# A chunked linear-attention layer in which every second 128-token tile lies backwards and two tiles share one score product per level

## The chip, the cores and the metric

The kernel runs on one core of one Trainium2 chip. The metric is the device time of one execution in microseconds. Engines are named as the profile names them: PE (TensorE matmul), PEld (TensorE weight load), DVE (VectorE), ACT (ScalarE), POOL (GpSimd), SP (SyncE, here the queue that issues most DMAs).

## The reference: what is computed

One layer of a hybrid decoder, for a prompt of 1024 tokens and for 8 sample sequences of 4 tokens, model width 1024, all in float32. After a norm, one wide projection feeds two branches: a gated linear recurrence (RG-LRU, 10 blocks of 128 channels, with a causal convolution of width 4), and gated linear attention (GLA, 4 heads, keys of 128, values of 256). Gates merge the branches; a SwiGLU feed-forward net follows. The attention is what the change touches; cut to the core it is

```python
bc = jnp.cumsum(gc, axis=2)
decay = jnp.exp(jnp.where(mask, bc[:, :, :, None, :] - bc[:, :, None, :, :], -jnp.inf))
att = jnp.einsum('bhik,bhjk,bhijk->bhij', qc, kc, decay)          # j <= i only
o = jnp.einsum('bhij,bhjv->bhiv', att, vc) + jnp.einsum('bhik,bhkv->bhiv', qc * jnp.exp(bc), S)
S = jnp.exp(b_last[:, :, 0, :])[..., None] * S + jnp.einsum('bhjk,bhjv->bhkv', kc * jnp.exp(b_last - bc), vc)
```

The decay differs for each of the 128 key channels, so the scores of a chunk are not one plain product of queries and keys. Any chunk length gives the same result.

## The kernel before

Features lie on the 128 partitions, tokens along the free dimension. The prompt is worked in two halves of 512 tokens one after the other, A (class `Half(0)`) and B (`Half(1)`), and the 32 sample tokens ride behind B's 512, so a row of B has 544 columns. A weight matrix is loaded tile by tile over SP's queue (`load_raw`, L125), split into a rounded part and the rest on ACT and DVE (`split_w`, L133), and multiplied in three products per tile (`gemm`, L342 to L357), of 512 columns in A and of twice 272 in B.

`branches` (L1184) sets the order by hand with generators: `mix` (L306) runs a main generator and, for each microsecond that it asks for with `yield`, takes as much from a fill generator. Main is the attention of a head pair (`gla`, L627); fill are the other projections and the RG-LRU (`lru_x` L900, `lru_gate` L931, `lru_g` L950). The instructions are then ordered by the framework's own scheduler under these priorities, at build time.

`gla` handles two heads at once and tiles of 128 tokens, four in a half. z, q and k are stored head by head (`qk`, L566), each with `N` columns (512 or 544). It goes like this:

- L634 to L642: log-decays, and their running sum `b_` by a scan that restarts at each tile (`rmask` holds 0 at a tile's first column).
- L646 to L655: `e0`, `qe` (queries times decay), `ke` (keys times what is left to the tile's end).
- L659 to L665: the diagonal of the scores, q·k at the same token, for eight tiles (`dps`), masked by the identity into `att`.
- Seven levels, `LEVELS = (64, 32, 16, 8, 4, 2, 1)`. At level b the tile is cut into blocks of b; each pair of neighbours has a lower block, whose tokens serve as keys, and an upper block, whose tokens serve as queries. With the decay at the pair's middle as the common reference, keys and queries each get one factor, and the score is a plain product. `lev_a` (L689) makes the differences to the middle (two DVE subtractions, L694 and L695) and their exponential (ACT, L696); `lev_b` (L699) multiplies by k and q (L700, L701); `lev_c` (L703) issues the products; `lev_d` (L729) puts the results in `att`, at levels 64 and 32 with copies on ACT (L739, L743), below with one masked copy on DVE (`copy_predicated`, L734). At levels 2 and 1, B's samples (4 tokens each) take part as well.
- `keys` (L679) transposes `ke`; then for each head and tile the output product (L777), the product with the state (L780), the state's update (L782, L791). In B the samples follow (L802 to L848).

The products of the levels from 16 down are these, one for each tile of each head, the whole tile as weights and its 64 queries as moving columns:

```python
for i in range(2):
    for t in range(4):
        c = i * N + t * P
        up = w[:, c:c + P].rearrange("p (s two b) -> p s two b", two=2, b=b)[:, :, 1, :]
        pe.matmul(sps[:, (4 * i + t) * 64:(4 * i + t + 1) * 64], w[:, c:c + P], up, start=True, stop=True)
```

Half of a tile's tokens are keys at a level and half are queries, but all 128 columns are loaded as weights.

Of the kernel before, what the change touches and what calls it, by code (L numbers as in the profile page):

```python
# [15 lines left out]
P = 128  # L16
# [26 lines left out]
def bc(ap, shape):  # L43
    return ap.to_broadcast(shape)


@with_exitstack
def hybrid_layer(ctx, tc, I, O):
# [51 lines left out]
    lmask = cp.tile([P, 7, 64], F32, name="lmask")  # L100
# [10 lines left out]
    rmask = cp.tile([P, 544], F32, name="rmask")  # L111
    pool.memset(rmask, 1.0)
    pool.memset(rmask[:, 0:HP:P], 0.0)
    pool.memset(rmask[:, HP:544:TS], 0.0)
# [200 lines left out]

    class Half:
        def __init__(s, hf):
            s.hf, s.N = hf, WID[hf]
            s.n = "ab"[hf]

            s.whole = (0, s.N, None, None)
            s.parts = [(0, 256, 0, 0), (256, 256, 0, 256)] if hf == 0 else [(0, 272, 0, 0), (272, 272, 1, 0)]
            s.adas = ada_rest() if hf == 0 else iter(())
            s.early = {}
            s.lr_raw = None
# [16 lines left out]
        def gemm(s, ps, hl, nk, rhs, k0=0, first=True, last=True, part=None, hk=0):  # L342
            N = s.N
            if part is None:
                pieces = [(0, HP, 0, 0)] if s.hf == 0 else s.parts
            else:
                pieces = [part]
            for kt in range(nk):
                x = rhs[k0 + kt]
                wh = hl[:, 0, (hk + kt) * P:(hk + kt + 1) * P]  # L350
                wl = hl[:, 1, (hk + kt) * P:(hk + kt + 1) * P]
                st, en = first and kt == 0, last and kt == nk - 1
                for o, w, bank, off in pieces:
                    out = ps[:, bank, off:off + w]
                    pe.matmul(out, wh, x[:, o:o + w], start=st, stop=False)  # L355
                    pe.matmul(out, wh, x[:, N + o:N + o + w], start=False, stop=False)  # L356
                    pe.matmul(out, wl, x[:, o:o + w], start=False, stop=en)  # L357
# [199 lines left out]
        def proj_h(s, t, name):  # L557
# [5 lines left out]
            s.gemm(ps, w_in_tile(t, name), KD, s.h)  # L563
            return ps

        def qk(s, pr, box):  # L566
            n, N = f"{s.n}{pr}", s.N
            z, q, k = S("z" + n), S("q" + n), S("k" + n)
            for i in range(2):
                ps = s.proj_h(T_Q + 2 * pr + i, f"qps{n}{i}")  # L570
                act.activation(s.sv(q[:, i * N:(i + 1) * N]), s.pv(ps), AF.Copy, scale=float(128 ** -0.5))
                yield 5.2
            for i in range(2):
                h = 2 * pr + i
                ps = mm(f"zps{n}{i}")
                for ci, (o, w) in enumerate(CHUNKS[s.hf]):
                    pe.matmul(ps[:, ci, :w], wa2[:, h, :], s.lrt[:, o:o + w], start=True, stop=True)
                act.activation(s.sv(z[:, i * N:(i + 1) * N]), s.pv(ps), AF.Identity, bias=vec[:, V_GBA + h:V_GBA + h + 1])
            yield 1.8
            for i in range(2):  # L580
                ps = s.proj_h(T_K + 2 * pr + i, f"kps{n}{i}")
                act.activation(s.sv(k[:, i * N:(i + 1) * N]), s.pv(ps), AF.Copy)
                yield 5.2
# [43 lines left out]
        def gla(s, pr, z, q, k, vg, vts):  # L627
# [20 lines left out]
            b3, k3 = hv(b_), hv(ke)  # L648
            bt = b3[:, :, :HP].rearrange("p h (t j) -> p h t j", j=P)
            dve.tensor_sub(k3[:, :, :HP].rearrange("p h (t j) -> p h t j", j=P), bc(bt[:, :, :, P - 1:P], [P, 2, 4, P]), bt)  # L650
            if s.hf:
                bs = b3[:, :, HP:].rearrange("p h (t j) -> p h t j", j=TS)
                dve.tensor_sub(k3[:, :, HP:].rearrange("p h (t j) -> p h t j", j=TS), bc(bs[:, :, :, TS - 1:TS], [P, 2, NB, TS]), bs)
# [13 lines left out]
            if s.hf:  # L667
                atts = tp.tile([NS, 64], F32, tag="atts", name="atts" + n, bufs=2)
                dps = ax(f"dpss{n}")
                for i in range(2):  # L670
                    c = i * N + HP
# [7 lines left out]
            def keys():  # L679
                for i in range(2):  # L680
                    tps = ax(f"ktp{n}{i}")
                    for t in range(4):
                        pe.transpose(tps[:, t * P:(t + 1) * P], ke[:, i * N + t * P:i * N + (t + 1) * P], ident)
                    act.activation(ktt[:, i * 512:(i + 1) * 512], tps, AF.Copy)

            def half(t, u, lim, b):
                return hv(t)[:, :, :lim].rearrange("p h (s two b) -> p h s two b", two=2, b=b)[:, :, :, u, :]

            def lev_a(li):  # L689
                b = LEVELS[li]  # L690
                w = S(f"w{n}{b}")[:, :W2]
                lim = N if s.hf and b <= 2 else HP
                mid = bc(half(b_, 0, lim, b)[:, :, :, b - 1:b], [P, 2, lim // (2 * b), b])
                dve.tensor_sub(half(w, 0, lim, b), mid, half(b_, 0, lim, b))  # L694
                dve.tensor_sub(half(w, 1, lim, b), half(b_, 1, lim, b), mid)  # L695
                act.activation(hv(w)[:, :, :lim], hv(w)[:, :, :lim], AF.Exp, scale=1.0 / 16)  # L696
                return w, b, lim

            def lev_b(w, b, lim):  # L699
                dve.tensor_mul(half(w, 0, lim, b), half(w, 0, lim, b), half(k, 0, lim, b))  # L700
                dve.tensor_mul(half(w, 1, lim, b), half(w, 1, lim, b), half(q, 1, lim, b))  # L701

            def lev_c(li, w, b, lim):  # L703
                sps = ax(f"sps{n}{b}")
                if b >= 32:

                    for i in range(2):
                        for t in range(4):
                            c, u = i * N + t * P, 4 * i + t
                            for g in (64 * (t % 2),) if b == 64 else (0, 64):  # L710
                                a, o = (c, u // 2 * b) if b == 64 else (c + g, u * b)
                                pe.matmul(sps[g:g + b, o:o + b], w[:, a:a + b], w[:, a + b:a + 2 * b], start=True, stop=True,
                                          skip_group_check=True)
                    return sps, None
                for i in range(2):
                    for t in range(4):
                        c = i * N + t * P
                        up = w[:, c:c + P].rearrange("p (s two b) -> p s two b", two=2, b=b)[:, :, 1, :]
                        pe.matmul(sps[:, (4 * i + t) * 64:(4 * i + t + 1) * 64], w[:, c:c + P], up, start=True, stop=True)
                s2 = None  # L720
                if lim > HP:
                    s2 = ax(f"sqs{n}{b}")
                    for i in range(2):
                        c = i * N + HP
# [4 lines left out]
            def lev_d(li, sps, s2):  # L729
                b = LEVELS[li]  # L730
                def put(dst, src, nq, nt, w):
                    dst = dst[:nq].rearrange("p (t s two b) -> p t s two b", t=nt, two=2, b=b)[:, :, :, 1, :]
                    msk = bc(lmask[:nq, li, :w].bitcast(I32).unsqueeze(1), [nq, nt, w])
# [3 lines left out]
                if b == 64:  # L737
                    for g in range(2):
                        act.activation(att[:64].rearrange("p (t j) -> p t j", t=8)[:, g::2, 64:],  # L739
                                       sps[64 * g:64 * g + 64, :256].rearrange("p (t j) -> p t j", t=4), AF.Copy)  # L740
                elif b == 32:
                    for g in (0, 64):
                        act.activation(att[g:g + 32].rearrange("p (t j) -> p t j", t=8)[:, :, g + 32:g + 64],  # L743
                                       sps[g:g + 32, :256].rearrange("p (t j) -> p t j", t=8), AF.Copy)
                else:
                    put(att, sps, P, 8, 64)
# [21 lines left out]
            for i in range(2):  # L768
# [4 lines left out]
                for t in range(4):  # L773
                    c = i * N + t * P
                    for v in range(2):
                        o = (po[v] if s.hf == 0 else po[:, v])[:, t * P:(t + 1) * P]
                        pe.matmul(o, vt[:, t * 256 + v * P:t * 256 + (v + 1) * P], att[:, (4 * i + t) * P:(4 * i + t + 1) * P],  # L777
# [4 lines left out]
                    pe.matmul(ups[:, :256], ktt[:, (4 * i + t) * P:(4 * i + t + 1) * P], vt[:, t * 256:(t + 1) * 256],  # L782
# [7 lines left out]
                    else:  # L790
                        dve.scalar_tensor_tensor(st, st_prev, e0[:, c + P - 1:c + P], ups[:, :256], op0=OP.mult, op1=OP.add)  # L791
# [10 lines left out]
                if s.hf:  # L802
# [3 lines left out]
                    kes = bc(ke[:, i * N + HP:i * N + N].unsqueeze(1), [P, 2, NS])  # L806
# [6 lines left out]
                                    qe[:, i * N + HP:i * N + N].rearrange("p (b j) -> p b j", j=TS))  # L813
# [20 lines left out]
                    for b in range(0, NB, 2):  # L834
# [3 lines left out]
                        for d in range(2):  # L838
                            sv = sts[(b + d) // 4][:, ((b + d) % 4) * 256:((b + d) % 4 + 1) * 256]
                            ec = i * N + HP + (b + d) * TS + TS - 1  # L840
# [59 lines left out]
        def lru_x(s, nb):  # L900
            N, n = s.N, f"{s.n}{nb}"
            ps = s.proj_h(T_UX + nb, "uxps" + n)
            buf = T("ub" + n, 576)
            if s.hf == 0:
                act.activation(buf[:, 3:3 + HP], ps[:, 0, :], AF.Copy)
            else:
                act.activation(buf[:, 3:275], ps[:, 0, :272], AF.Copy)
                act.activation(buf[:, 275:515], ps[:, 1, :240], AF.Copy)
                sb = buf[:, 515:571].rearrange("p (b t) -> p b t", t=7)
                act.activation(sb[:, :, 3:7], ps[:, 1, 240:272].rearrange("p (b t) -> p b t", t=TS), AF.Copy)  # L910
# [39 lines left out]
        def lru_g(s, nb, beta, a, ti):  # L950
# [21 lines left out]
            dve.scalar_tensor_tensor(gg[:, :N], hh, 0.5, gg[:, :N], op0=OP.mult, op1=OP.mult)  # L972
# [293 lines left out]

def _pack(inp):
# [5 lines left out]
    a["xa"] = c(_feat(xp[:HP]).reshape(P, -1))  # L1273
    a["xb"] = c(_feat(np.concatenate([xp[HP:], xs], 0)).reshape(P, -1))
# [35 lines left out]
    a["lmask"] = np.stack([((jj // (2 * b) == ii // b) & (jj % (2 * b) < b)) for b in LEVELS], 1).astype(np.float32)  # L1310
# [30 lines left out]
```

## Time and profile before

| what | value |
|---|---|
| median of 3 runs | 2039.98 us (2039.82 to 2040.99) |
| span of the profiled execution | 2038.1 us |
| PE busy | 2003.7 us |
| DVE busy | 1093.7 us |
| ACT busy | 802.5 us |
| POOL busy | 76.3 us |
| mean granted TensorE clock | 0.995 of full |
| HBM traffic over the span | 111 GB/s |

The span runs from the first to the last instruction on the core; the device time has a little around it. "Busy" is the time in which an engine had at least one instruction under way. Matmuls are pipelined and overlap, so the mean length of one is not what one costs: that is read from how far apart they start. An fp32 product is recorded as two weight loads and two matmuls. In names of tiles, a final a or b stands for the half (`spsa`: the level products of half A).

### The profile page before, as it was taken

What the parts mean: (1) busy time and instruction counts of PE and PEld (TensorE: products, weight loads), DVE (VectorE), ACT (ScalarE), POOL (GpSimd) and SP (SyncE); (2) the same over time, 40 slices, a digit from 0 to 9 for tenths busy, and PEclk for the clock granted to TensorE, in tenths of its full rate; (3) what the DMA queues carried; (4) which work ended last, traced back from release to release, by engine and by line L of the source; (5) the groups of instructions that cost most, each with busy time, mean ns of one, the idle gap of its engine ahead of it and who ended that gap; (6) DMA issues with size and microseconds to landing.
All of it is one profiled execution on the core that took longest, in us unless ns stands there. A gap on an engine that the chain in (4) does not pass through costs nothing. (4 is left out here: it accounts for less than half of the span.)

```text
span 2038.1 us, 31898 instructions
## 1 busy us (share of the span) xinstructions
PE 2003.7 (98%) x13370; PEld 1804.6 (89%) x13370; DVE 1093.7 (54%) x1764; ACT 802.5 (39%) x1129; POOL 76.3 (4%) x130
## 2 busy tenths in 40 slices
PE   8999999999999999999999999999999999999997
PEld 5887877777899888888899999999999999999997
DVE  5647486544357433446473687764433773333446
ACT  3535375533235322233352455653323442222232
POOL 0101001000000000000010101010000000000000
PEclk9999999999999999999999999999999999999998
DMA  8324233334344323232422313223223542232243
GB/s 306 106 91 132 81 105 104 112 114 155 95 164 155 115 85 111 95 137 85 142 73 86 117 53 104 99 88 104 80 85 114 173 135 84 72 105 94 81 121 123
DMA packets 74639, 228.41 MB, mean 112 GB/s; under 512 B 8704, under 2 KB 16768, under 8 KB 74496
## 3 DMA queue, kind: packets, MB, share of 16 engines
q1 hardware_dynamic: 71536, 217.38, 33.0%
q0 software_dynamic: 2416, 8.44, 1.1%
q8 instruction: 105, 1.72, 0.4%
q10 hardware_dynamic: 544, 0.56, 0.1%
q14 instruction: 38, 0.31, 0.0%
HBM read 217.11 MB, written 9.23 MB: 111 GB/s over the span
## 5 line engine op out<-in xcount | busy, mean ns | idle before, releaser
L357 PE MATMUL f3psb<-fab,f3b_hl 128*128 128x272 f32 x352 | 101.4, 288 | 0.0
L355 PE MATMUL f3psb<-fab,f3b_hl 128*128 128x272 f32 x352 | 101.3, 288 | 0.0
L356 PE MATMUL f3psb<-fab,f3b_hl 128*128 128x272 f32 x352 | 100.9, 287 | 0.0
L136 ACT ACTIVATE f3b_hl<-f3b_raw 128x768 fp32r<-128x768 f32 (+1 forms) x45 | 35.7, 793 | 88.5 <-PE f3psb L357 57.2
L355 PE MATMUL f3psa<-faa,f3a_hl 128*128 128x512 f32 x176 | 68.7, 390 | 0.0
L357 PE MATMUL f3psa<-faa,f3a_hl 128*128 128x512 f32 x176 | 68.5, 389 | 0.0
L356 PE MATMUL f3psa<-faa,f3a_hl 128*128 128x512 f32 x176 | 68.5, 389 | 0.0
L355 PEld LDWEIGHTS f3psb<-fab,f3b_hl 128*128 128x128 f32 x352 | 66.4, 189 | 0.0
L357 PEld LDWEIGHTS f3psb<-fab,f3b_hl 128*128 128x128 f32 x352 | 66.2, 188 | 0.0
L356 PEld LDWEIGHTS f3psb<-fab,f3b_hl 128*128 128x128 f32 x352 | 66.1, 188 | 0.0
L137 DVE TENSOR_TENSOR f3b_hl<-f3b_raw,f3b_hl 128x768 fp32r<-128x768 f32 (+1 forms) x45 | 40.1, 891 | 35.1 <-ACT f3b_hl L136 35.0
L136 ACT ACTIVATE f3a_hl<-f3a_raw 128x768 fp32r<-128x768 f32 (+1 forms) x32 | 25.4, 793 | 84.1 <-PE f3psa L357 47.7
L137 DVE TENSOR_TENSOR f3a_hl<-f3a_raw,f3a_hl 128x768 fp32r<-128x768 f32 (+1 forms) x32 | 28.5, 891 | 38.9 <-ACT f3a_hl L136 38.2
L355 PE MATMUL uxpsb<-h1b,uxpsb_hl 128*128 128x272 f32 x160 | 47.5, 297 | 0.1
L357 PE MATMUL uxpsb<-h1b,uxpsb_hl 128*128 128x272 f32 x160 | 46.6, 291 | 0.0
L356 PE MATMUL uxpsb<-h1b,uxpsb_hl 128*128 128x272 f32 x160 | 46.2, 289 | 0.0
L355 PE MATMUL ugpsb<-h1b,ugpsb_hl 128*128 128x272 f32 x160 | 46.2, 289 | 0.0
L357 PE MATMUL ugpsb<-h1b,ugpsb_hl 128*128 128x272 f32 x160 | 46.1, 288 | 0.0
L356 PE MATMUL ugpsb<-h1b,ugpsb_hl 128*128 128x272 f32 x160 | 45.8, 286 | 0.0
L357 PEld LDWEIGHTS f3psa<-faa,f3a_hl 128*128 128x128 f32 x176 | 33.0, 188 | 7.1 <-DVE f3a_hl L137 0.2
L355 PEld LDWEIGHTS f3psa<-faa,f3a_hl 128*128 128x128 f32 x176 | 33.0, 188 | 6.8
L356 PEld LDWEIGHTS f3psa<-faa,f3a_hl 128*128 128x128 f32 x176 | 33.0, 188 | 6.8
(1483 smaller groups left out, 7122.9 us busy)
## 6 DMA issues: line engine op xcount, KB each, us to landing
ada<-in_ada_w SPq DMA_DIRECT2D x48, 512.0 KB, 5.5
f3b_raw<-in_ffn SPq DMA_DIRECT2D x23, 384.0 KB, 3.1
f3b_raw<-in_ffn SPq DMA_DIRECT2D x22, 320.0 KB, 2.9
woa_raw<-in_w_out SPq DMA_DIRECT2D x13, 512.0 KB, 3.5
wob_raw<-in_w_out SPq DMA_DIRECT2D x13, 512.0 KB, 3.3
f3a_raw<-in_ffn SPq DMA_DIRECT2D x16, 384.0 KB, 3.1
uxpsa_raw<-in_w_in SPq DMA_DIRECT2D x10, 512.0 KB, 3.6
ugpsa_raw<-in_w_in SPq DMA_DIRECT2D x10, 512.0 KB, 3.6
```

The lines of the kernel that those rows point to most:

```text
L136: act.activation(hl[:, 0, :n], raw[:, :n], AF.Copy)
L137: dve.tensor_sub(hl[:, 1, :n], raw[:, :n], hl[:, 0, :n].bitcast(F32))
L355: pe.matmul(out, wh, x[:, o:o + w], start=st, stop=False)
L356: pe.matmul(out, wh, x[:, N + o:N + o + w], start=False, stop=False)
L357: pe.matmul(out, wl, x[:, o:o + w], start=False, stop=en)
```

## The change

Tokens of a half are stored in another order: the four tiles 0, 1, 2, 3 lie as 0, 2, then 1 and 3 with their 128 tokens backwards. The host lays the inputs out so and puts the outputs back. z, q and k of a head pair are stored as 512 columns of forward tiles (two tiles of either head), 512 columns of backward tiles, and in B the samples of both heads behind them. In a backward tile, what is a lower block stands where a forward tile has its upper one. So at each level, of a forward tile and a backward tile that stand at the same place, the keys of the one and the keys of the other fill 128 columns together; they become one weight tile, the queries of both become 128 moving columns in two runs of 64, and the result is written in two runs of 64, one for each tile. What of the product pairs one tile's keys with the other's queries is masked out.

With it go: one scan forward over the first 512 columns and one backward over the second, in B a third for the samples; two masked copies instead of one at each level from 16 down; at level 32 four copies instead of two; in B separate instructions for the samples at levels 2 and 1, and on ACT for q, z and k; in B the q, z, k and convolution projections cut at 256 and 288 columns instead of twice 272; the convolution's input and the gated output of the RG-LRU put back to and from time order, in pieces of 256. The yields that order the work are unchanged.

The diff, cut to its core:

```diff
+def at(t, off, *dims):
+    one = t[:, off:off + 1]
+    return bass.AP(one.tensor, one.offset, [list(one.ap[0])] + [list(d) for d in dims])
...
+    def in_time(t, u):
+        return t[:, :HP].rearrange("p (m u n) -> p m u n", u=2, n=P)[:, :, u, :]
...
+            s.tiled = None if hf == 0 else [(0, 256, 0, 0), (256, 288, 1, 0)]
...
-                pieces = [(0, HP, 0, 0)] if s.hf == 0 else s.parts
+                pieces = split or ([(0, HP, 0, 0)] if s.hf == 0 else s.parts)
...
+        def by_tiles(s, dst, i, ps, func, **kw):
+            d = dst[:, :1024].rearrange("p (u n) -> p u n", u=2)[:, :, i * 256:(i + 1) * 256]
+            if s.hf == 0:
+                act.activation(d, ps[:, 0, :].rearrange("p (u n) -> p u n", u=2), func, **kw)
+            else:
+                act.activation(d, ps[:, :, :256], func, **kw)
+                act.activation(dst[:, 1024 + i * NS:1024 + (i + 1) * NS], ps[:, 1, 256:288], func, **kw)
...
-                act.activation(s.sv(q[:, i * N:(i + 1) * N]), s.pv(ps), AF.Copy, scale=float(128 ** -0.5))
+                s.by_tiles(q, i, ps, AF.Copy, scale=float(128 ** -0.5))
...
-            for i in range(2):
-                dve.tensor_tensor_scan(b_[:, i * N:(i + 1) * N], rmask[:, :N], z[:, i * N:(i + 1) * N], 0.0,
-                                       op0=OP.mult, op1=OP.add)
+            scan = lambda out, x, m: dve.tensor_tensor_scan(out, m, x, 0.0, op0=OP.mult, op1=OP.add)
+            scan(b_[:, :512], z[:, :512], rmask[:, :512])
+            scan(b_[:, 512:1024][:, ::-1], z[:, 512:1024][:, ::-1], rmask[:, :512])
+            if s.hf:
+                scan(b_[:, 1024:], z[:, 1024:], rmask[:, HP:HP + 2 * NS])
...
+            def keys_at(t, b):
+                return at(t, 0, (2 * b, 256 // b), (512 + b, 2), (1, b))
+
+            def queries_at(t, b):
+                return at(t, b, (512 - b, 2), (2 * b, 256 // b), (1, b))
+
+            def packed(w, b):
+                return at(w, 0, (2 * b, 256 // b), (b, 2), (1, b)), at(w, 512, (256, 2), (b, 256 // b), (1, b))
...
-                dve.tensor_sub(half(w, 0, lim, b), mid, half(b_, 0, lim, b))
-                dve.tensor_sub(half(w, 1, lim, b), half(b_, 1, lim, b), mid)
-                act.activation(hv(w)[:, :, :lim], hv(w)[:, :, :lim], AF.Exp, scale=1.0 / 16)
+                wk, wq = packed(w, b)
+                dve.tensor_sub(wk, at(b_, b - 1, (2 * b, 256 // b), (513, 2), (0, b)), keys_at(b_, b))
+                dve.tensor_sub(wq, queries_at(b_, b), at(b_, b - 1, (513, 2), (2 * b, 256 // b), (0, b)))
+                if lim > 1024:
+                    mid = bc(smp(b_, 0, b)[:, :, b - 1:b], [P, NS // b, b])
+                    dve.tensor_sub(smp(w, 0, b), mid, smp(b_, 0, b))
+                    dve.tensor_sub(smp(w, 1, b), smp(b_, 1, b), mid)
+                act.activation(w[:, :lim], w[:, :lim], AF.Exp, scale=1.0 / 16)
...
+                wk, wq = packed(w, b)
+                dve.tensor_mul(wk, wk, keys_at(k, b))
+                dve.tensor_mul(wq, wq, queries_at(q, b))
...
-                for i in range(2):
-                    for t in range(4):
-                        c = i * N + t * P
-                        up = w[:, c:c + P].rearrange("p (s two b) -> p s two b", two=2, b=b)[:, :, 1, :]
-                        pe.matmul(sps[:, (4 * i + t) * 64:(4 * i + t + 1) * 64], w[:, c:c + P], up, start=True, stop=True)
+                both = lambda t: t.rearrange("p (u n) -> p u n", u=2)
+                for e in range(4):
+                    pe.matmul(both(sps)[:, :, e * 64:(e + 1) * 64], w[:, e * P:(e + 1) * P],
+                              both(w[:, 512:1024])[:, :, e * 64:(e + 1) * 64], start=True, stop=True)
...
-                    put(att, sps, P, 8, 64)
+                    for u in range(2):
+                        put(att[:, u * 512:(u + 1) * 512], sps[:, u * 256:(u + 1) * 256], P, 4, 64, u)
...
+            for u in range(2):
+                src = (ps[:, 0, u * 256:(u + 1) * 256] if s.hf == 0 else ps[:, u, :256]).rearrange("p (m n) -> p m n", m=2)
+                act.activation(in_time(buf[:, 3:3 + HP], u), src[:, :, ::-1] if u else src, AF.Copy)
...
-            dve.scalar_tensor_tensor(gg[:, :N], hh, 0.5, gg[:, :N], op0=OP.mult, op1=OP.mult)
+            for u in range(2):
+                g2 = gg[:, u * 256:(u + 1) * 256].rearrange("p (m n) -> p m n", m=2)
+                h2 = in_time(hh, u)
+                dve.scalar_tensor_tensor(g2, h2[:, :, ::-1] if u else h2, 0.5, g2, op0=OP.mult, op1=OP.mult)
+            if s.hf:
+                dve.scalar_tensor_tensor(gg[:, HP:N], hh[:, HP:], 0.5, gg[:, HP:N], op0=OP.mult, op1=OP.mult)
```

More of the change, by code (lines that the diff above doesn't have):

```diff
@@ L99, in hybrid_layer @@
     pool.dma_start(ident, I["ident"])
-    lmask = cp.tile([P, 7, 64], F32, name="lmask")
+    lmask = cp.tile([P, 5, P], F32, name="lmask")
     bmask = cp.tile([P, NB], F32, name="bmask")
@@ L110, in hybrid_layer @@
     pool.memset(ones, 1.0)
-    rmask = cp.tile([P, 544], F32, name="rmask")
+    rmask = cp.tile([P, 576], F32, name="rmask")
     pool.memset(rmask, 1.0)
     pool.memset(rmask[:, 0:HP:P], 0.0)
-    pool.memset(rmask[:, HP:544:TS], 0.0)
+    pool.memset(rmask[:, HP:576:TS], 0.0)
     hist = cp.tile([P, NR, 3], F32, name="hist")
@@ L340, in psv, with gemm @@
             return s.pv(ps) if part[2] is None else ps[:, part[2], part[3]:part[3] + part[1]]
-        def gemm(s, ps, hl, nk, rhs, k0=0, first=True, last=True, part=None, hk=0):
+        def gemm(s, ps, hl, nk, rhs, k0=0, first=True, last=True, part=None, hk=0, split=None):
             N = s.N
             if part is None:
-                pieces = [(0, HP, 0, 0)] if s.hf == 0 else s.parts
+                pieces = split or ([(0, HP, 0, 0)] if s.hf == 0 else s.parts)
             else:
@@ L575, in qk @@
                 ps = mm(f"zps{n}{i}")
-                for ci, (o, w) in enumerate(CHUNKS[s.hf]):
+                for o, w, ci, off in s.tiled or [(0, HP, 0, 0)]:
                     pe.matmul(ps[:, ci, :w], wa2[:, h, :], s.lrt[:, o:o + w], start=True, stop=True)
-                act.activation(s.sv(z[:, i * N:(i + 1) * N]), s.pv(ps), AF.Identity, bias=vec[:, V_GBA + h:V_GBA + h + 1])
+                s.by_tiles(z, i, ps, AF.Identity, bias=vec[:, V_GBA + h:V_GBA + h + 1])
             yield 1.8
             for i in range(2):
-                ps = s.proj_h(T_K + 2 * pr + i, f"kps{n}{i}")
-                act.activation(s.sv(k[:, i * N:(i + 1) * N]), s.pv(ps), AF.Copy)
+                ps = s.proj_h(T_K + 2 * pr + i, f"kps{n}{i}", s.tiled)
+                s.by_tiles(k, i, ps, AF.Copy)
                 yield 5.2
@@ L682, in keys, with smp @@
                     for t in range(4):
-                        pe.transpose(tps[:, t * P:(t + 1) * P], ke[:, i * N + t * P:i * N + (t + 1) * P], ident)
+                        pe.transpose(tps[:, t * P:(t + 1) * P], ke[:, i * 512 + t * P:i * 512 + (t + 1) * P], ident)
                     act.activation(ktt[:, i * 512:(i + 1) * 512], tps, AF.Copy)
-            def half(t, u, lim, b):
-                return hv(t)[:, :, :lim].rearrange("p h (s two b) -> p h s two b", two=2, b=b)[:, :, :, u, :]
+            def smp(t, u, b):
+                return t[:, 1024:1088].rearrange("p (s two b) -> p s two b", two=2, b=b)[:, :, u, :]
@@ L693, in lev_a @@
-                mid = bc(half(b_, 0, lim, b)[:, :, :, b - 1:b], [P, 2, lim // (2 * b), b])
-                dve.tensor_sub(half(w, 0, lim, b), mid, half(b_, 0, lim, b))
-                dve.tensor_sub(half(w, 1, lim, b), half(b_, 1, lim, b), mid)
-                act.activation(hv(w)[:, :, :lim], hv(w)[:, :, :lim], AF.Exp, scale=1.0 / 16)
+                w = S(f"w{n}{b}")
+                lim = 1088 if s.hf and b <= 2 else 1024
+                wk, wq = packed(w, b)
+                dve.tensor_sub(wk, at(b_, b - 1, (2 * b, 256 // b), (513, 2), (0, b)), keys_at(b_, b))
@@ L701, in lev_b @@
-                dve.tensor_mul(half(w, 1, lim, b), half(w, 1, lim, b), half(q, 1, lim, b))
+                wk, wq = packed(w, b)
+                dve.tensor_mul(wk, wk, keys_at(k, b))
+                dve.tensor_mul(wq, wq, queries_at(q, b))
+                if lim > 1024:
+                    dve.tensor_mul(smp(w, 0, b), smp(w, 0, b), smp(k, 0, b))
+                    dve.tensor_mul(smp(w, 1, b), smp(w, 1, b), smp(q, 1, b))
             def lev_c(li, w, b, lim):
@@ L705, in lev_c @@
                 if b >= 32:
-                    for i in range(2):
-                        for t in range(4):
[L709 to L713, printed above, removed]
-                    return sps, None
-                for i in range(2):
-                    for t in range(4):
-                        c = i * N + t * P
-                        up = w[:, c:c + P].rearrange("p (s two b) -> p s two b", two=2, b=b)[:, :, 1, :]
-                        pe.matmul(sps[:, (4 * i + t) * 64:(4 * i + t + 1) * 64], w[:, c:c + P], up, start=True, stop=True)
+                    for e in range(4):
+                        for r in range(0, P, b):
+                            u, g = r // b % 2, e * 64 // b + r // (2 * b)
+                            pe.matmul(sps[r:r + b, e * b:(e + 1) * b], w[:, e * P + r:e * P + r + b],
+                                      w[:, 512 + 256 * u + g * b:512 + 256 * u + (g + 1) * b], start=True, stop=True,
+                                      skip_group_check=True)
+                    return sps, None
+                both = lambda t: t.rearrange("p (u n) -> p u n", u=2)
+                for e in range(4):
+                    pe.matmul(both(sps)[:, :, e * 64:(e + 1) * 64], w[:, e * P:(e + 1) * P],
+                              both(w[:, 512:1024])[:, :, e * 64:(e + 1) * 64], start=True, stop=True)
                 s2 = None
-                if lim > HP:
+                if lim > 1024:
                     s2 = ax(f"sqs{n}{b}")
                     for i in range(2):
-                        c = i * N + HP
+                        c = 1024 + i * NS
                         up = w[:, c:c + NS].rearrange("p (s two b) -> p s two b", two=2, b=b)[:, :, 1, :]
@@ L730, in lev_d, with put @@
                 b = LEVELS[li]
-                def put(dst, src, nq, nt, w):
-                    dst = dst[:nq].rearrange("p (t s two b) -> p t s two b", t=nt, two=2, b=b)[:, :, :, 1, :]
-                    msk = bc(lmask[:nq, li, :w].bitcast(I32).unsqueeze(1), [nq, nt, w])
+                def put(dst, src, nq, nt, w, u=0):
+                    dst = dst[:nq].rearrange("p (t s two b) -> p t s two b", t=nt, two=2, b=b)[:, :, :, 1 - u, :]
+                    msk = bc(lmask[:nq, li - 2, u * 64:u * 64 + w].bitcast(I32).unsqueeze(1), [nq, nt, w])
                     dve.copy_predicated(dst, msk.rearrange("p t (s b) -> p t s b", b=b),
                                         src.rearrange("p (t s b) -> p t s b", t=nt, b=b))
[L737 to L744, printed above, removed]
-                else:
-                    put(att, sps, P, 8, 64)
+                if b >= 32:
+                    for r in range(0, P, b):
+                        u = r // b % 2
+                        c = r + b * (1 - 2 * u)
+                        act.activation(att[r:r + b, u * 512:(u + 1) * 512].rearrange("p (e j) -> p e j", e=4)[:, :, c:c + b],
+                                       sps[r:r + b, :4 * b].rearrange("p (e j) -> p e j", e=4), AF.Copy)
+                else:
+                    for u in range(2):
+                        put(att[:, u * 512:(u + 1) * 512], sps[:, u * 256:(u + 1) * 256], P, 4, 64, u)
                 if s2 is not None:
@@ L781, in gla @@
                     ups = ax(f"ups{n}{i}{t}")
-                    pe.matmul(ups[:, :256], ktt[:, (4 * i + t) * P:(4 * i + t + 1) * P], vt[:, t * 256:(t + 1) * 256],
+                    pe.matmul(ups[:, :256], ktt[:, c:c + P], vt[:, u * 256:(u + 1) * 256],
                               start=True, stop=True)
@@ L790, in gla @@
                     else:
-                        dve.scalar_tensor_tensor(st, st_prev, e0[:, c + P - 1:c + P], ups[:, :256], op0=OP.mult, op1=OP.add)
+                        ec = c if t % 2 else c + P - 1
+                        dve.scalar_tensor_tensor(st, st_prev, e0[:, ec:ec + 1], ups[:, :256], op0=OP.mult, op1=OP.add)
                     st_prev = st
@@ L1264, in _feat, with _stored @@
     return x.T.reshape(f // P, P, t).transpose(1, 0, 2)
+def _stored():
+    import numpy as np
+    t = np.arange(HP).reshape(4, P)
+    return np.concatenate([t[0], t[2], t[1][::-1], t[3][::-1]])
 def _pack(inp):
@@ L1309, in _pack @@
     ii = np.arange(64)[None, :]
-    a["lmask"] = np.stack([((jj // (2 * b) == ii // b) & (jj % (2 * b) < b)) for b in LEVELS], 1).astype(np.float32)
+    a["lmask"] = np.stack([np.concatenate([((jj // (2 * b) == ii // b) & (jj // b % 2 == u)) for u in range(2)], 1)
+                           for b in LEVELS[2:]], 1).astype(np.float32)
     a["bmask"] = (np.arange(P)[:, None] % NS // TS == np.arange(NB)[None, :]).astype(np.float32)
```

51 lines of the change are left out of this document (23 added, 28 removed).

## The prediction

> **What bounds the kernel now.** I read the page first: its span, the busy times and the row of slices.
>
> ```profile
> span 2038.1 us, 31898 instructions
> PE 2003.7 (98%) x13370; PEld 1804.6 (89%) x13370; DVE 1093.7 (54%) x1764; ACT 802.5 (39%) x1129; POOL 76.3 (4%) x130
> PE   8999999999999999999999999999999999999997
> ```
>
> TensorE has work in 98% of the span, VectorE in about half. The profiled execution spans 2038.1 us and the median of the runs is 2039.98 us, so 1.9 us lie around the span; I sum against the span and add the same to the median. Busy matmuls overlap, so the next question is what TensorE waits for: the view of waits, for TensorE, in the stretch of half B's branches (1000 to 1400 us) and, first row, of half A's (60 to 340 us).
>
> ```profile
> PE rpsoa L374 <- DVE atta L664: 3.5, 1, 3.5
> ...
> PE spsb L712 <- DVE wb L701: 2.3, 1, 2.3
> PE g1b L937 <- DVE mbb L1026: 1.2, 1, 1.2
> PE pob L780 <- DVE stb L791: 1.1, 1, 1.1
> ```
>
> The columns are total us, times and longest. Where the change works, TensorE waits for 3.5 us in A and 4.6 us in these rows of B. So TensorE's own instructions set the time there, and each microsecond taken from its queue should shorten the span, if VectorE keeps up.
>
> **What the merged products are worth.** A level of 16 or less issues one product for each of 8 tiles of two heads, now: 128 weight columns, 64 moving columns. Each fp32 product is two records, so a level is 16. The change issues four products with 128 moving columns, 8 records. The groups by line and form hold 160 records in each half, 5 levels of 16 in each of two head pairs:
>
> ```profile
> L719 PE MATMUL spsa<-wa 128*128 128x64 f32 x160 | 19.5, 275 | 0.0
> L719 PE MATMUL spsb<-wb 128*128 128x64 f32 x160 | 18.9, 271 | 0.0
> ```
>
> Busy us, then the mean ns of one; the records overlap. The timeline shows one such level, its weight loads (PEld) and matmuls (PE), and the 16 records of the diagonal products, which have the new shape (128 weight columns, 128 moving columns):
>
> ```profile
> 97.99 1.86 PEld L719 LDWEIGHTS spsa<-wa 128*128 128x128 f32 x16 [0.41 <-issue]
> 97.99 2.00 PE L719 MATMUL spsa<-wa 128*128 128x64 f32 x16
> ...
> 66.27 1.98 PEld L663 LDWEIGHTS dpsa<-qa,ka 128*128 128x128 f32 x16
> 66.49 1.95 PE L663 MATMUL dpsa<-qa,ka 128*128 128x128 f32 x16
> ```
>
> Columns: start, length, engine and line, then count. One record lasts 275 ns, so 16 that start s apart take 15 s + 0.275 us: (2.00 − 0.275)/15 = 115 ns. For the diagonal, with twice the moving columns: (1.95 − 0.275)/15 = 112 ns. So a record costs 112 ns whether 64 or 128 columns move. What both have alike is the load of 128 weight columns, which fills the same time (1.86 and 1.98 us for 16), and the change halves the loads. Per level 8 records go, 8 × 0.112 = 0.90 us. There are 5 such levels, 2 head pairs and 2 halves, 20 in all: 17.9 us, half in A, half in B. The groups bound it: 19.5 + 18.9 = 38.4 us of busy time with the tail of each level counted; half is 19.2 us, an upper end. The lower end is nothing (rivals).
>
> The Trainium skill speaks against this. "TensorE: Matmul & The Clock Gate", section "Back-to-back issue gap", gives an isolated matmul about 60 cycles up to 64 moving columns and 134 at 128, by which two narrow products cost no more than one wide one and the sum would be 0. The rows disagree: 115 and 112 ns.
>
> **The rest of TensorE's work.** Levels 64 and 32 keep their 16 and 32 records. Level 32 writes to four strips of 32 rows where it wrote to two.
>
> ```profile
> 80.33 0.69 PE L712 MATMUL spsa<-wa 128*64 128x64 f32 x16
> 87.05 0.70 PE L712 MATMUL spsa<-wa 128*32 128x32 f32 x32
> ```
>
> 32 records take 0.70 us now. With four strips they could overlap twice as well (−0.35 us each of four times, −1.4) or cost as much each as the 64-wide (+0.7 each, +2.8). I take 0, the row of its own shape.
>
> In B the q, k and conv projections move 256 and 288 columns where they moved 272 twice: 18 tiles × 8 × 3 = 432 pairs. Windows that hold only one width:
>
> ```profile
> 1400.00:1440.00 40.00, 40.00 (x323) 40.00 (x323) 12.73 (x13) 11.08 (x14) 0.00 (x0) 1.00 0.24 80
> 590.00:600.00 10.00, 10.00 (x86) 10.00 (x85) 4.62 (x10) 2.73 (x5) 0.00 (x0) 1.00 0.57 183
> 900.00:910.00 10.00, 10.00 (x46) 8.29 (x45) 7.73 (x10) 6.19 (x10) 0.00 (x0) 1.00 0.34 128
> ```
>
> (Length; PE, PEld, DVE, ACT, POOL busy with counts; clock; DMA.) 272 columns: 40.00/323 = 124 ns; 256: 10.00/86 = 116; 512: 10.00/46 = 217. From 272 to 512 that is 6 ns for 16 columns, so 288 cost 130 and the pair 246 against 248; with the two records cut by the window's edges taken off, 119, 125 and 131 give 250 against 250. Between −0.9 and +0.6 us; I take 0.
>
> **VectorE and ScalarE.** What is added is instructions, hardly elements. Durations:
>
> ```profile
> L695 DVE TENSOR_TENSOR wa<-bca x14: 675/683/689, 76.0 to 211.5; 128x512 f32<-128x512 f32 x14
> ```
>
> (minimum, median and maximum ns, over all levels), and by groups:
>
> ```profile
> L650 DVE TENSOR_TENSOR kea<-bca 128x1024 f32<-128x1024 f32 x2 | 2.4, 1222 | 0.0
> L673 DVE TENSOR_TENSOR attsb<-dpssb,ident 32x64 f32<-32x64 f32 x2 | 0.4, 209 | 0.3 <-PE dpssb L672 0.3
> L927 DVE SCALAR_TENSOR_TENSOR xcb<-ubb,vec,cvb 128x32 f32<-128x32 f32 x10 | 2.5, 245 | 0.0
> L905 ACT ACTIVATE uba<-uxpsa 128x512 f32<-128x512 f32 x10 | 6.0, 597 | 29.7 <-PE uxpsa L357 29.7
> L907 ACT ACTIVATE ubb<-uxpsb 128x272 f32<-128x272 f32 x10 | 3.9, 393 | 22.5 <-PE uxpsb L357 22.5
> L910 ACT ACTIVATE ubb<-uxpsb 128x32 f32<-128x32 f32 x10 | 2.1, 206 | 0.0
> ```
>
> 512 more elements cost 0.54 us, so an instruction's fixed part is 0.14. Each masked copy becomes two (5 × 0.14 = 0.7 us a head pair). B's two sample levels get four small instructions each of about 0.2, less the 0.04 that each big one loses (1.3), and a third scan (0.2). The gate product becomes two in A (+0.14 × 10) and three in B (0.14 + 0.2, × 10). VectorE: A 2 × 0.7 + 1.4 = 2.8 us, B 2 × 2.2 + 3.4 = 7.8. ScalarE: the conv input in two pieces in A (2 × 0.39 − 0.60 = 0.2, × 10), B's samples of q, z and k apart (12 × 0.2), four copies of 128 columns for level 32 instead of two of 256 (at 0.8 ns a column from the two rows of 272 and 32: 4 × 0.28 − 2 × 0.38 = 0.4, × 4): about 6 us. No DMA moves in any queue; POOL's products keep their size.
>
> New patterns have no row: reversed scans and reads, and at level 1 a read that jumps half a tile at every element. A bound from a neighbour, the masked copy at level 4 and at level 2 (runs of 4 and 2 elements in what it writes):
>
> ```profile
> 1210.15 0.70 DVE L734 COPY_PREDICATED attb<-lmask,spsb 128x512 f32<-128x512 int32 x1 [1.76 <-PE spsb L719]
> 1213.77 1.31 DVE L734 COPY_PREDICATED attb<-lmask,spsb 128x512 f32<-128x512 int32 x1 [0.42 <-PE spsb L719]
> ```
>
> Short runs nearly double that one, while the subtractions of L695 take 675 to 689 ns at every level. I take no penalty; at worst 0.6 us on the two key instructions of levels 1 and 2, 2.4 us a head pair, and 1.2 on two scans, 3.6 together.
>
> **What hides it.** In the second head pair of B, how far is VectorE ahead? Its last instruction for a level (L701) and TensorE's first product of that level, for levels 64, 8 and 1:
>
> ```profile
> 1178.28 0.67 DVE L701 TENSOR_TENSOR wb<-wb,qb 128x512 f32<-128x512 f32 x1
> 1179.10 0.69 PE L712 MATMUL spsb<-wb 128*64 128x64 f32 x16 [2.33 <-DVE wb L701]
> ...
> 1187.84 0.67 DVE L701 TENSOR_TENSOR wb<-wb,qb 128x512 f32<-128x512 f32 x1
> 1200.45 1.89 PE L719 MATMUL spsb<-wb 128*128 128x64 f32 x16
> ...
> 1204.99 0.72 DVE L701 TENSOR_TENSOR wb<-wb,qb 128x544 f32<-128x544 f32 x1
> 1221.81 1.89 PE L719 MATMUL spsb<-wb 128*128 128x64 f32 x16
> ```
>
> Only level 64 starts as VectorE ends; level 8 has 11.9 us in hand, level 1 has 16.1. TensorE gains 4.5 us on it over a head pair and VectorE loses 2.2: the lead holds. Before level 64, what the change adds is exposed: a scan and a sample copy, 0.4 us, in B at least once; I take 0.5 us. The tightest stretch by windows:
>
> ```profile
> 1160.00:1180.00 20.00, 17.66 (x152) 16.78 (x151) 19.80 (x28) 11.77 (x15) 6.78 (x4) 1.00 0.09 27
> 1180.00:1200.00 20.00, 20.00 (x191) 19.81 (x191) 19.09 (x32) 10.14 (x15) 0.00 (x0) 1.00 0.14 41
> 1200.00:1220.00 20.00, 20.00 (x155) 19.28 (x155) 15.83 (x28) 13.12 (x22) 1.70 (x8) 1.00 0.31 93
> 1220.00:1240.00 20.00, 18.86 (x151) 18.34 (x151) 14.72 (x24) 9.92 (x13) 3.93 (x9) 1.00 0.29 86
> ```
>
> VectorE is busy for 69.4 of 80 us. With 2.2 for the levels and about 1 for the gates it needs 72.6 of the 75.5 that are left: it fits, by 2.9 us, but 38.9 of the first 40 are taken. I let a third of the 4.5 us saved in this pair be lost to VectorE, an estimate: 1.5 us. In A nothing is lost.
>
> Last, two short stretches run at half clock:
>
> ```profile
> 174.00:178.00 4.00, 4.00 (x24) 2.56 (x22) 3.97 (x7) 2.14 (x3) 0.00 (x0) 0.57 0.08 12
> 1293.60:1300.50 6.90, 6.90 (x24) 5.97 (x24) 3.37 (x10) 2.70 (x5) 0.00 (x0) 0.51 0.37 138
> ```
>
> 0.43 × 4.0 = 1.7 us and 0.49 × 6.9 = 3.4 us of work are lost there. The first follows the 3.5 us wait for L664. A shifted order can lose these stretches (−5.1) or meet another (+3.4). I take them as they are.
>
> **Sum:** −17.9 + 0 + 0 + 0.5 + 1.5 = −15.9 us: a span of 2022.2 and a time of 2024.1 us, said as 2024.
>
> **Rivals.** First, VectorE's queue becomes the bound in B: the short runs cost their worst (3.6 us a pair on top of 2.2) and the saved time turns into waits for L701 and the masked copies. For it: 19.8 and 19.09 of 20. Against: the leads of 12 and 16 us. All of B's 8.9 us would go: 2039.98 − 17.9 + 8.9 + 0.5 = 2031.5. Chance 0.16.
>
> Second, the change doesn't do what it says on the array: a product costs by its moving columns, two narrow and one wide alike. For it only that no product with its moving operand in two runs is in the trace; against it the 115 and 112 ns. Nothing saved, 0.5 lost: 2040.5. Chance 0.06. It is also what the gap table of the skill would give.
>
> Third, slower: the wide product writes its result in two runs of 64 columns, 1 KB apart in PSUM, which no product in the trace does, and is slowed by it. 160 records are left, so the gain is gone at 224 ns a record, and beyond 224 + 4.1/0.16 = 250 ns it is a loss that shows. At 336 ns, three times the row, it is 160 × 0.112 = 17.9 us slower: 2057.9 (2058). Against: the moving reads come in runs of 8 at level 8 and of 1 at level 1, and both levels take the same 1.89 us; runs of 64 are long beside that. Chance 0.04. The Trainium skill, "Advanced Engine Details and Errata", section "Memory Cachelines", says that any non-contiguous pattern in PSUM slows matmuls significantly, and that every two consecutive elements should adjoin. The second half of it excuses runs of 64; no run here shows either.
>
> **How the numbers follow.** The forecast has 0.74, with its own range 2017 (the full 17.9 and both half-clock stretches gone: 2039.98 − 17.9 − 5.1) to 2029. Up to the first rival's 2031.5, with 2.8 more for level 32 in strips, is 2034: low 2017, high 2034. About 1 in 6 is left out: the two rivals above, and a little beyond each end. 0.2% of the time, 4.1 us, is about what a measurement of this kernel can tell from no change. Forecast and first rival are faster by more: 0.89, given its tails, I say 0.88; the second is the same: 0.07; slower 0.05.
>
> **What would show it.** The line of L719's successor has 80 records in each half with the mean near 275 ns, 8 in a row in some 1.06 us ((7 × 0.112) + 0.275). PE's busy total falls by 16 to 18 us and stays at 98% of the span. A level's first product still starts many us after VectorE's last for that level. Masked copies come in pairs of 0.4 to 0.8 us. It would be wrong if wide products start 150 ns or more apart, if TensorE's waits for VectorE in 1000 to 1400 us grow from the 4.6 us above to over 10 us, or if the tensor subtractions at level 1 pass 1 us and their products follow them at once.

## The result and the profile after

The changed kernel takes 2024.16 us, median of four runs (2020.9 to 2025.3), against 2039.99 us for the kernel before (2039.82 to 2040.99): a ratio of 0.9918, 95% interval 0.9905 to 0.993. The profiled execution spans 2023.1 us, 15.0 us less than before. The page after, its first two lines:

```profile
span 2023.1 us, 31697 instructions
PE 1990.7 (98%) x13210; PEld 1789.0 (88%) x13210; DVE 1098.6 (54%) x1832; ACT 804.6 (40%) x1159; POOL 77.5 (4%) x130
```

PE has 160 matmul records fewer and 13.0 us less of busy time; its share stays at 98%. VectorE gained 68 instructions and only 4.9 us. The merged products, by line and form, and one level of them in the timeline (start, length, engine, count), with level 32 above it:

```profile
L753 PE MATMUL spsa<-wa 128*128 128x128 f32 x80 | 11.4, 283 | 0.0
L753 PE MATMUL spsb<-wb 128*128 128x128 f32 x80 | 10.6, 275 | 0.0
```

```profile
86.56 0.46 PE L747 MATMUL spsa<-wa 128*32 128x32 f32 x32
106.36 1.06 PE L753 MATMUL spsa<-wa 128*128 128x128 f32 x8
```

Eight records take 1.06 us, so they start (1.06 − 0.275)/7 = 112 ns apart. Five levels of half A, of the twenty in all, take 1.16 us, 126 ns a record. The 16 records with half the moving columns took 1.89 us in most levels of before, (1.89 − 0.275)/15 = 108 ns apart, and up to 2.00 us, 115 ns, in the others. So twice the moving columns cost 4 to 11 ns a record. The result in two runs of 64 columns costs nothing that shows: the diagonal's product, with 128 moving columns and one run, was at 112 ns too. The groups' busy time fell from 38.4 to 22.0 us, 16.4. Level 32, in four strips, takes 0.46 us instead of 0.70.

What TensorE waits for, half A's branches in the first row, half B's in the others:

```profile
PE rpsoa L384 <- DVE atta L684: 3.5, 1, 3.5
...
PE spsb L747 <- DVE wb L735: 2.0, 1, 2.0
PE pob L815 <- DVE stb L827: 1.4, 2, 0.9
PE opsb L372 <- DVE oacb L892: 0.9, 2, 0.5
PE g1b L972 <- ACT lab L979: 0.9, 1, 0.9
```

The two large waits of before stand, 3.5 and 2.0 us (2.3 before). All of TensorE's idle time, span less busy, is 32.4 us against 34.4, and 33.7 and 35.0 in the two profiled runs of the same kernel below: no wait grew out of the saved time that can be told from this spread. VectorE is still ahead of the products. In half B's second head pair its last instruction for level 8 and for level 1, and TensorE's first product of each:

```profile
1174.97 0.68 DVE L735 TENSOR_TENSOR wb<-wb,qb 128x512 f32<-128x512 f32 x1
1187.42 1.05 PE L753 MATMUL spsb<-wb 128*128 128x128 f32 x8
...
1193.45 0.68 DVE L735 TENSOR_TENSOR wb<-wb,qb 128x512 f32<-128x512 f32 x1
1207.05 1.06 PE L753 MATMUL spsb<-wb 128*128 128x128 f32 x8
```

That is a lead of 11.8 us at level 8 (11.9 before) and of 12.9 us at level 1 (16.1 before).

Last, the windows in which the granted clock (third column from the end) is half, outside the first 20 and the last 10 us:

```profile
168.00:172.50 4.50, 4.07 (x20) 2.63 (x21) 4.48 (x7) 2.14 (x3) 0.00 (x0) 0.62 0.04 15
1165.00:1169.00 4.00, 3.60 (x27) 3.51 (x28) 4.00 (x7) 3.30 (x6) 0.00 (x0) 0.57 0.02 6
1278.00:1285.00 7.00, 6.76 (x22) 5.83 (x23) 3.57 (x12) 2.61 (x5) 0.00 (x0) 0.51 0.40 149
1612.70:1616.10 3.40, 3.40 (x16) 3.40 (x17) 2.72 (x8) 1.29 (x3) 0.00 (x0) 0.50 0.43 167
```

Before had two such stretches. These lose 0.38 × 4.5 + 0.43 × 4.0 + 0.49 × 7.0 + 0.50 × 3.4 = 8.6 us of full clock; the two before lost 1.7 + 3.4 = 5.1. One more, of 3.4 us, lies in the first 20 us of the changed kernel.

### The profile page after: what moved, and what is told of

Its sections match the earlier page's. It is cut to its first block, busy times and chain, and to the rows that moved or that the text cites. A ratio compares the mean times of both kernels' runs of the same rounds, so it can differ in the third digit from the quotient of the medians.

```text
span 2023.1 us, 31697 instructions
## 1 busy us (share of the span) xinstructions
PE 1990.7 (98%) x13210; PEld 1789.0 (88%) x13210; DVE 1098.6 (54%) x1832; ACT 804.6 (40%) x1159; POOL 77.5 (4%) x130
## 4 chain that ended last, share of the span: by engine, by line
PE 87%; DVE 5%; DMA 4%; ACT 2%; issue 1%; SPq 0%; DVEq 0%; ACTq 0%
PE f3psb L365 2%; PE f3psb L367 2%; PE f3psb L366 2%; PE f3psa L365 2%; PE f3psa L367 2%; PE f3psa L366 2%; DMA ada<-in_ada_w 2%; PE papsb L365 1%; PE papsb L367 1%; PE papsb L366 1%; PE papsa L366 1%; PE papsa L367 1%; PE papsa L365 1%; PE adaps L199 1%; PE uxpsa L367 1%
## 5 line engine op out<-in xcount | busy, mean ns | idle before, releaser
L365 PE MATMUL uxpsb<-h1b,uxpsb_hl 128*128 128x256 f32 (+1 forms) x160 | 47.7, 298 | 0.1
L366 PE MATMUL uxpsb<-h1b,uxpsb_hl 128*128 128x256 f32 (+1 forms) x160 | 46.3, 289 | 0.0
L367 PE MATMUL uxpsb<-h1b,uxpsb_hl 128*128 128x256 f32 (+1 forms) x160 | 46.2, 289 | 0.0
```

## The experiments

Theory: a level's product costs the load of its 128 weight columns, about 112 ns a record; the merge halves the loads, and VectorE's added work is covered by its lead over the products. Rivals: the moving columns are what is paid, so the gain comes from elsewhere in the new layout; or VectorE's queue is near enough to being the bound that part of the gain went to it.

**Narrow products in the new layout.** Everything of the change stays, but each product is issued as two with the same weights:

```diff
 for e in range(4):
-    pe.matmul(both(sps)[:, :, e * 64:(e + 1) * 64], w[:, e * P:(e + 1) * P],
-              both(w[:, 512:1024])[:, :, e * 64:(e + 1) * 64], start=True, stop=True)
+    for u in range(2):
+        pe.matmul(both(sps)[:, u, e * 64:(e + 1) * 64], w[:, e * P:(e + 1) * P],
+                  both(w[:, 512:1024])[:, u, e * 64:(e + 1) * 64], start=True, stop=True)
```

> The changed kernel with its layout and all its added instructions, but each merged product issued as two products of 64 moving columns with the same 128 weight columns: 8 products (16 records) a level again. If the load of 128 weight columns is what a record costs, 160 records come back at 112 ns, 17.9 us: about 2042 us, level with the kernel before or up to 2 us above it, and 16 records of a level take 1.9 us. If a product costs by its moving columns, nothing changes: about 2024 us.

**Wide products, issued twice.** The same number of records, twice the moving columns:

```diff
 for e in range(4):
-    pe.matmul(both(sps)[:, :, e * 64:(e + 1) * 64], w[:, e * P:(e + 1) * P],
-              both(w[:, 512:1024])[:, :, e * 64:(e + 1) * 64], start=True, stop=True)
+    for again in range(2):
+        pe.matmul(both(sps)[:, :, e * 64:(e + 1) * 64], w[:, e * P:(e + 1) * P],
+                  both(w[:, 512:1024])[:, :, e * 64:(e + 1) * 64], start=True, stop=True)
```

> The changed kernel with each merged product issued twice, 128 moving columns each time: 160 records more. If the weight load is the cost, the same 17.9 us as for the two narrow products: about 2042 us, and no difference between these two kernels beyond 2 us. If the moving columns are the cost, this one alone pays: some 18 us more than the one with two narrow products.

Measured: 2038.65 us with narrow products (2037.27 to 2040.93, ratio to before 0.9998, 0.9988 to 1.0007) and 2039.08 us with doubled ones (2036.97 to 2042.76, ratio 0.9998, 0.9989 to 1.0008), against 2024.08 for the changed kernel on the same chip. One level in the timeline, narrow and then doubled:

```profile
108.54 1.89 PE L754 MATMUL spsa<-wa 128*128 128x64 f32 x16
```

```profile
108.22 1.95 PE L754 MATMUL spsa<-wa 128*128 128x128 f32 x16
```

Sixteen records take 1.89 us with 64 columns and 1.95 with 128, 108 and 112 ns apart, and the two kernels are alike in time. The whole gain is the halved number of records; the layout by itself is worth nothing that can be told from zero. Both came back by some 15 us, not the 17.9 expected. TensorE's busy time is 15.4 us longer with narrow products than in the changed kernel profiled beside it (2003.6 against 1988.2), though the narrow one had less half clock outside its last stretch (10.2 us against 13.7, which is 1.7 us of work): about 17 us in all. The theory of columns has fallen. That it is the load of 128 weight columns, and not some other price of a record, stays argued, for no run changes the weight columns alone. What speaks for it are the level-64 products, where 16 records with 64 weight columns take 0.69 us; but they go to two strips of output rows and may overlap.

**Every masked copy twice.**

```diff
-for u in range(2):
+for u in (0, 1, 0, 1):
     put(att[:, u * 512:(u + 1) * 512], sps[:, u * 256:(u + 1) * 256], P, 4, 64, u)
```

> The changed kernel with every masked copy of the levels done twice: 40 copies more at 0.44 us (24 of them) or 0.79 us (16), 23 us of VectorE, 5.8 us in each head pair. If VectorE's lead of 5 to 17 us over the products hides what was added, the time moves by less than 2 us: 2022 to 2027 us. If VectorE is the bound in half B's branches, half B pays most of its share: 2030 to 2036 us.

**Every masked copy four times**, with `(0, 1) * 4` in the same place.

> The changed kernel with every masked copy done four times: 69 us of VectorE more, 17 us in each head pair, which is more than its lead of 5 to 17 us over the products. If the lead is what hides VectorE's work, the cover ends here: waits of TensorE for VectorE appear in the branches of half B above all, and the time is 2030 to 2055 us. If VectorE has slack beyond the lead, it stays within 4 us of the changed kernel, under 2028 us.

Doubled: 2026.42 us (2025.43 to 2027.99), 2.3 us over the changed kernel beside it (2024.08), a little over the 2 us that the theory allowed and far from the rival's 6 to 12; the ranges overlap. TensorE's idle time did not grow (32.8 us, against 33.7 in the changed kernel beside it). VectorE's busy time rose by 16.8 us, from 1098.6 to 1115.4, not by 23: copies that follow one another overlap. Four times: 2039.24 us (2033.86 to 2042.61), all of the gain gone, with 50 us more of VectorE instead of the 69 expected and 42.7 us of idle time on TensorE. Its waits in half B, and the tightest window (length; PE, PEld, DVE, ACT, POOL busy; clock):

```profile
PE pob L812 <- DVE attb L769: 3.5, 1, 3.5
...
PE spsb L753 <- DVE attsb L769: 1.8, 2, 1.1
```

```profile
1220.00:1240.00 20.00, 15.43 (x108) 14.42 (x108) 18.93 (x39) 6.62 (x10) 1.47 (x7) 0.91 0.10 34
```

The copies now stand directly ahead of the product that reads `att`, and TensorE is idle for 4.6 of 20 us there. So the lead does cover the change's own VectorE work, and the cover ends somewhere between one and three more sets of copies. Half clock adds to the loss (mean clock 0.991 to 0.994 in these ten runs).

**The changed kernel again**, twice, beside the others.

> The changed kernel once more, to see what its spread is (2020.9 to 2025.3 us in four runs). If stretches of half clock make it, time follows the mean granted clock: each stretch of 3.4 us costs 1.7 us and 0.0008 of the mean clock, so runs at 0.995 lie near 2021 us and runs at 0.992 near 2025 or 2026 us. If not, times scatter without regard to the clock.

> The changed kernel beside it on the same chip, for the difference: 2021 to 2026 us, whatever the cause of the waits.

Measured: 2024.08 us (2023.2 to 2027.11) and 2023.33 us (2021.2 to 2027.37). Over all 13 runs of the changed kernel the time goes with the clock: a mean of 2026.2 us for the two at 0.992, 2026.6 for three at 0.993, 2023.5 for four at 0.994, 2022.5 for three at 0.995, 2021.2 for one at 0.996. The kernel before does the same: 2042.3 us at 0.992 (three runs), 2037.7 at 0.996 (ten). From 0.992 to 0.996 that is 5.0 and 4.6 us, where half clock on busy work would cost 0.004 × 2025 = 8. The mean clock also counts the last stretch, of 7.6 us in the profiled run, in which TensorE is busy for 0.05 us. So most of the spread (6.5 us in the changed kernel) goes with half clock, and the number of its stretches differs from run to run of one program: outside the last there are five, three and five in the three profiled runs of the changed kernel.

**Without POOL's products.** The two large waits follow places where VectorE is slow. The timeline of VectorE and then of POOL in half A of the changed kernel:

```profile
160.09 2.55 DVE L142 TENSOR_TENSOR rpsa_hl<-rpsa_raw,rpsa_hl 128x1024 fp32r<-128x1024 f32 x1 [0.47 <-ACT rpsa_hl L141]
162.57 2.87 DVE L723 TENSOR_TENSOR wa<-bca 128x512 f32<-128x512 f32 x1
165.36 0.68 DVE L724 TENSOR_TENSOR wa<-bca 128x512 f32<-128x512 f32 x1
```

```profile
159.19 2.38 POOL L668 TENSOR_TENSOR qea<-qa,e0a 128x1024 f32<-128x1024 f32 x1 [84.19 <-ACT e0a L667]
161.53 3.37 POOL L675 TENSOR_TENSOR kea<-kea,ka 128x1024 f32<-128x1024 f32 x1
```

The subtraction L723 takes 2.87 us where its median is 0.68, and ends 0.5 us after POOL does. The edit moves POOL's work to VectorE:

```diff
-pool.tensor_mul(qe, q, e0)
+dve.tensor_mul(qe, q, e0)
...
-pool.tensor_mul(ke, ke, k)
+dve.tensor_mul(ke, ke, k)
```

> The changed kernel with the two products that POOL makes in each head pair (queries and keys by their decays, 2.4 to 3.6 us each) made by VectorE instead, at about 1.2 us each. While POOL makes them, VectorE's subtraction of a level takes 2.9 us instead of 0.7 and a weight split 2.5 instead of 1.2, and just there TensorE waits 3.5 us in half A (for the diagonal's copy) and 2.0 us in half B (for the first level), each with a half-clock stretch on its heels. If the slowed VectorE makes these waits, they shrink to under 1 us each, the half-clock stretches behind them go, and the time falls by 4 to 8 us to 2016 to 2020 us. If the waits come from the order of VectorE's queue alone, its 10 us of added work leave them or make them longer: 2024 us or more.

Measured: 2016.09 us (2014.89 to 2019.22), ratio to the kernel before 0.9885 (0.9871 to 0.9898), 7.2 us under the changed kernel beside it. Its page, its wait in half A, and VectorE at the same place:

```profile
PE 1983.0 (99%) x13210; PEld 1782.7 (89%) x13210; DVE 1093.0 (54%) x1840; ACT 804.9 (40%) x1159; POOL 52.9 (3%) x122
```

```profile
PE rpsoa L384 <- DVE atta L684: 0.9, 1, 0.9
```

```profile
161.92 1.21 DVE L142 TENSOR_TENSOR rpsa_hl<-rpsa_raw,rpsa_hl 128x1024 fp32r<-128x1024 f32 x1
163.05 1.22 DVE L675 TENSOR_TENSOR kea<-kea,ka 128x1024 f32<-128x1024 f32 x1
```

VectorE does eight instructions more and is busy 5.6 us less. The wait of 3.5 us, for the second copy of the diagonal, is gone; the 0.9 us in its row is a new wait for the first copy, which now stands behind a product that was POOL's. The one of 2.0 us for the first level of half B is gone from the list, and the mean clock of the profiled run is 0.997. The scheduler also moved the second diagonal copy ahead of L723 in VectorE's queue, so how much of the lost wait is the slowing and how much the order stays open. Half clock is much of the gain: against the changed kernel profiled beside it, a pair that lies 11.9 us apart, TensorE's idle time is 4.9 us less and its busy time 7.0 us less, and of 20.5 us of half clock outside the last stretch none is left. That these stretches went because the waits did was expected, and fits, but is not shown. "SBUF — State Buffer" of the Trainium skill, section "Terms", says that VectorE and GpSimd arbitrate for a pair of ports and that the loser is blocked for the other's whole instruction; the 2.87 us beside POOL's 3.37 agree with that.

**The same edit in the kernel before.**

> The kernel before, with POOL's two products of each head pair made by VectorE. If POOL's slowing of VectorE and the waits behind it have nothing to do with the new layout, the old kernel gains much as the new one did (7 us of 2023): its waits of 3.5 and 2.3 us and its half-clock stretch at 174 us go, 2032 to 2037 us. If the new layout made them cost more, the old one gains less than 3 us: over 2037 us.

Measured: 2032.91 us (2031.39 to 2038.11), 6.9 us under the kernel before, ratio 0.9968 (0.9952 to 0.9983). Here the profiled run gained by idle time, 28.7 us against 34.4, and hardly by busy time (2003.1 against 2003.7). The gains of the two edits add up within their intervals: with POOL's products on VectorE in both, the merge is worth 2032.91 − 2016.09 = 16.8 us, measured on two chips. These runs lie at clocks of 0.994 to 0.997, the highest here, so half clock disturbs this measure of the change least.

## Why the prediction was right, point by point

**The bound and the merged products: right, a little oversized.** 2024 us was predicted and 2024.16 measured, and the step that carried it, that a record of 128 weight columns costs about the same whether 64 or 128 columns move, was shown three ways: in the timeline after, and by the narrow and the doubled products. The term was −17.9 us. PE's busy time fell by 13.0, short of the 16 to 18 named as a sign. The changed kernel lost some 5 us more to half clock than the one before (20.5 us in such stretches outside the last one, the first 20 us counted, by their starts and lengths in the trace, against 10.2, at half speed), which leaves about −18 of work. Level 32 gave 0.24 us four times, −1.0, where 0 was taken and −1.4 bounded it, so the products gave about −17. The term was a little too large because the 115 ns of the narrow records was read from a slow level; most levels had 108.

**The waits: 2.0 us too many.** 0.5 us before the first level and 1.5 us lost to VectorE in half B were added. Neither came: the wait for L735 is 2.0 us against 2.3 for its forerunner, and TensorE's waits from 1000 to 1400 us come to 6.4 us against 6.3. The step that failed is the size of VectorE's added work, from which both terms were drawn: 2.8 + 7.8 = 10.6 us were counted, and its busy time rose by 4.9. A split instruction was given a fixed part of 0.14 us each time. The masked copies, before and after, show what it is:

```profile
L734 DVE COPY_PREDICATED atta<-lmask,spsa 128x512 f32<-128x512 int32 x10 | 9.5, 953 | 15.3 <-PE spsa L719 15.2
L734 DVE COPY_PREDICATED attb<-lmask,spsb 128x512 f32<-128x512 int32 x10 | 9.6, 962 | 23.9 <-PE spsb L719 23.9
...
L769 DVE COPY_PREDICATED atta<-lmask,spsa 128x256 f32<-128x256 int32 x20 | 10.1, 562 | 9.2 <-PE spsa L753 9.2
L769 DVE COPY_PREDICATED attb<-lmask,spsb 128x256 f32<-128x256 int32 x20 | 10.1, 564 | 14.2 <-PE spsb L753 14.2
```

20.2 us for forty against 19.1 for twenty: two that follow one another overlap, and twice as many cost 1.1 us more, not 2.8.

**The half-clock stretches: not foreseen in size.** They were taken as they are, with −5.1 to +3.4 as bounds. In the profiled run they cost about 5 us more than before, which is outside these bounds; over all runs the mean clock is 0.9938 (13 runs) against 0.9945 for the kernel before (43 runs), which is 0.0007 × 2025 = 1.4 us. In the profiled pair −17 of products, −1 of level 32, +5 of clock and −2 of idle time make the −15.0 between the spans, where the prediction had −17.9 + 2.0 = −15.9. That the time was met so closely was luck in these small terms; its size came from the products.

**The rivals.** VectorE as the bound: not reached by the change; it begins somewhere between one and three more sets of masked copies. Cost by moving columns: refuted. The write in two runs: 112 ns a record, refuted. And the penalty for short runs in the key subtractions is small. It shows at level 1 alone, where the read jumps at every element. That level is the last of the seven of a head pair; its subtraction in the changed kernel, and the rows (minimum, median and maximum ns) of all levels in half A there and in the kernel without POOL's products:

```profile
105.77 0.83 DVE L723 TENSOR_TENSOR wa<-bca 128x512 f32<-128x512 f32 x1
...
L723 DVE TENSOR_TENSOR wa<-bca x14: 678/684/2881, 72.7 to 200.7; 128x512 f32<-128x512 f32 x14
L723 DVE TENSOR_TENSOR wa<-bca x14: 678/682/840, 74.7 to 197.1; 128x512 f32<-128x512 f32 x14
```

The 2881 is the one beside POOL; without it the longest is level 1, at 840 ns against a median of 682. So 0.15 us, where 0 was taken and 0.6 was the worst case.

## What to carry to other kernels

When TensorE is always busy, count products and the weight tiles they load: here an fp32 product with 64 moving columns cost 108 ns a record and one with 128 cost 112, so a layout that fills the weight tile and the moving side with twice the useful columns nearly halves the cost of the step. Check what such a layout adds to another engine against that engine's lead over the products, not against its mean share of busy time. And look at what stands just ahead of an unexplained wait: here two products per head pair on a nearly idle engine cost some 7 us, close to half of what the merge gains.

## What was not expected of the hardware

- Two POOL products of 2.4 to 3.6 us in each head pair, a 4% busy engine, made a VectorE subtraction take 2.87 us instead of 0.68; moving them to VectorE took 6.9 us off the old kernel and 7.2 off the new one, in the new one largely as half clock that was gone.
- Half-clock stretches last 3.4 or 6.8 us and their number changes from run to run of one program; mean clocks of 0.992 and 0.996 lie 4.6 us (before) and 5.0 us (changed) apart. That a stretch follows a long wait fits the two at 174 and 169 us and their going with the waits, but the longest waits just before those at 1278 and 1612 us of the changed kernel are 0.5 and 0.6 us, so what sets them off is not settled here.
- Level 32 in four strips of 32 output rows runs its 32 records in 0.46 us, in two strips in 0.70.
